# Block products in both MLPs of a two-layer decoder trunk, with the S5 preparation rewritten to run beside them

## The chip, the cores and the metric

One core of one Trainium2 chip runs the whole program. The metric is the device time of one execution in microseconds (us). Median of three runs of the kernel before: 2741.39 us (2741.0 to 2742.24).

## The reference, cut to what matters

Two layers on a sequence of 1024 tokens with 1024 channels. Layer 0 mixes tokens by retention, layer 1 by an S5 state-space layer, and each is followed by an MLP of 2816 inner columns with a causal convolution of width 3 on its gate.

```python
def conv_ffn(h, w_up, conv_w, conv_b, w_down):
    val, gate = jnp.split(h @ w_up, 2, axis=-1)
    gate = lax.conv_general_dilated(gate, conv_w, window_strides=(1,), padding=[(CONV_W - 1, 0)], ...) + conv_b
    return (jax.nn.silu(gate) * val) @ w_down

def reference(x, c, pos, ...):
    ...
        h = rms_norm(x) * (1.0 + sc1) + sh1
        ...                                      # i = 0: retention_mixer, i = 1: s5_mixer
        x = x + g1 * y
        h = rms_norm(x) * (1.0 + sc2) + sh2
        x = x + g2 * conv_ffn(h, ffn_w_up[i], ffn_conv_w[i], ffn_conv_b[i], ffn_w_down[i])
    return rms_norm(x) * final_norm_g
```

The S5 mixer's matrices (powers of complex numbers, cosines and sines of angles) depend on the parameters alone, so they can be prepared while something else runs.

## The kernel before

**Arithmetic.** Every f32 factor is split in a high and a low half, and a product is three TensorE products: high by high, high by low, low by high (`mm3`, L802 to L805). ACT copies the high half of a weight (`whi`), VectorE subtracts it for the low half (`wlo`). A matmul here is a 128x128 block of weights against 512 tokens (128x512).

**Stages in program order.** Retention projection and mixer; MLP 0 from about 917 us; the S5 mixer; MLP 1 from 2025.3 us; final norm. Channels lie on partitions, tokens on the free axis, in two halves of 512.

**MLP 0, plain** (`ffn_plain`, L1629). The 2816 inner columns are 22 pairs of 128 (gate and value). For a pair, gate and value times both token halves are four products of 24 matmuls, 96 in all. `gate_out` copies the gate into the convolution's buffer E, `val_out` does the convolution (L1659 to L1661), silu, product and split (L1668). The down-projection follows in groups of two pairs, nine times, and at last four pairs at once.

**MLP 1, block products** (`ffn`, L1769). The up-projection of a pair is regarded as a 2x2 block product (two halves of the input channels, two halves of the tokens) and done by seven products of 12 matmuls, 84 in all, on sums of blocks: A11, S2, S3, S1, A22, A12, S4 (`Q7`; `pair`, L1821). The activation's sums (`SB.b1`, `SB.t1` and so on) are made once, at normalisation (`steps_s`, L666 to L758, which makes `hs`). After each product `tt` (L1248, VectorE) adds or subtracts its bank: into `u` or `tu`, E, or `t`. The first five pairs (`LEADS`) run while the second token half is still being normalised: two of their seven products were done ahead (`lead`), so five are left. The activations are stored in DRAM (`ff_d`) and loaded again for the down-projection, which goes in six groups (`GROUPS`).

**Weights** come through one queue, class `Stream` (L199). `loads` issues DMAs from SP into raw buffers `wr` (three, plus in MLP 1 one "bonus", `wra`, and one lent, `wrx`, while slots are free). `advance` (L270) makes the block sums: two loads into temporaries (`s1`, `s2`), then four adding DMAs issued by POOL (L284, L285, L287 for two). `split` (L338) makes the halves: ACT copy L368, VectorE subtraction L369 for a block; L354 and L355 for a whole weight of the plain kind. `step`, once per product, moves all of it on:

```python
        def step(self):
            self.now += 1
            self.pump()
            self.pump()
```

**S5 preparation** (`s5_weights`, L1380) is a Python generator in the list `bgq`; every `bg()` issues what stands up to its next `yield`. In MLP 0 it is called in the middle of each product (`mid=bg`) and after it (`tick`). It goes over eight groups in two halves. A half group: two multiplies and an add on POOL (`outer`, the add L128 `ar<-ar`), an angle product and two wraps on POOL (`sev<-sp,cst`, L1424, L1425), four transposes on TensorE (L1429), the angle reduction on VectorE (L1433, L1435, L836, L1437), two sines on ACT, `outer` again, four small products (L1451), and stores. After two halves the block is read back in another order and stored (`t_d`). `p1_d`, `cs_d`, `w1_d`, `t_d` are its outputs, `ar` and `sev` its buffers; `ar` and `aacc` have the same sizes as the temporaries of the block sums.

**Banks.** TensorE writes to eight banks `bk`. `RA` counts them round in MLP 0 and the norms, `ffn` has a counter of its own, `DB`.

## Time and profile before

| | |
|---|---|
| median of three runs | 2741.39 us |
| the profiled execution | 2736.73 us |
| its span, first to last instruction | 2734.6 us |
| TensorE's mean granted clock (1 is full) | 0.992 |
| MLP 0 begins, S5 mixer begins, MLP 1 begins | about 917, 1690, 2025.3 us |
| S5 preparation in MLP 0 | 951 to 1536 us |

The profile names for each engine the time in which it was busy; PE is TensorE, PEld its weight load (which goes on beside the products), DVE VectorE, ACT ScalarE, POOL GpSimd, SP the engine that issues most loads. A row of a view of waits gives the waiting engine and line, what it waited for, the sum, the number of times and the longest. A row of the view of instructions gives line, engine, operation, output and inputs with sizes, the number, and busy time with the mean of one; behind the second bar the idle time before them with who ended it. All rows are from the profiled execution.

### The profile page before, as it was taken

To read this page: it belongs to the slowest core of one execution; us is meant where nothing else is said; L and a number is where in the kernel's file an instruction comes from. 1 tells how busy PE (TensorE), PEld (TensorE's weight loads), DVE (VectorE), ACT (ScalarE), POOL (GpSimd) and SP (SyncE) were. 2 spreads that over 40 slices of the span, in tenths; PEclk is the share of its full clock that TensorE was granted. 3 is DMA by queue.
4 is the path that set the end of the run, shared out by engine and by line. 5 is a ranking of instruction groups with operands and counts; after the bars stand their busy time and mean duration, and the time that the engine had idled before them with its cause. 6 is when DMAs were issued, how large, how long until landed. Compare 5 with 4: busy or idle time off the path is not lost.

```text
span 2734.6 us, 33612 instructions
## 1 busy us (share of the span) xinstructions
PE 2647.9 (97%) x13041; PEld 2224.5 (81%) x13041; DVE 1627.4 (60%) x2254; ACT 856.4 (31%) x1346; POOL 847.3 (31%) x718
## 2 busy tenths in 40 slices
PE   6999999999999999999999999999998999999998
PEld 4798888888888778888888888888876788888887
DVE  8664564755765775666666545664247666666454
ACT  5322131231321343333333223222245434343112
POOL 5445676776100423333333004221122212110004
PEclk8999999999999999999999999999999999999999
DMA  7644335343432132332323213995247866645211
GB/s 246 165 135 143 112 119 165 113 154 116 128 135 77 37 100 82 100 100 92 100 96 100 80 45 123 298 288 168 70 114 167 203 159 165 170 125 207 101 61 62
DMA packets 341819, 357.12 MB, mean 131 GB/s; under 512 B 40444, under 2 KB 279580, under 8 KB 341660
## 3 DMA queue, kind: packets, MB, share of 16 engines
q1 hardware_dynamic: 292028, 269.36, 31.8%
q10 hardware_dynamic: 36960, 62.55, 6.4%
q0 software_dynamic: 12672, 23.07, 4.9%
q8 instruction: 102, 1.67, 0.2%
q14 instruction: 57, 0.47, 0.1%
HBM read 259.82 MB, written 70.42 MB: 121 GB/s over the span
## 4 chain that ended last, share of the span: by engine, by line
PE 74%; DVE 11%; DMA 5%; ACT 4%; issue 2%; POOL 2%; SPq 1%; ACTq 0%; POOLq 0%; DVEq 0%
PE bk L803 23%; PE bk L805 23%; PE bk L804 22%; PE bk L1115 1%; PE bk L1113 1%; PE bk L1114 1%; DVE wlo L355 1%; DMA U<-u_d 1%; POOL ar L128 1%; ACT whi L354 1%; DVE stf L1188 1%; DMA blk<-in_ada_w 1%; PE bk L2181 1%; DVE bacc L497 1%; PE bk L1209 1%
## 5 line engine op out<-in xcount | busy, mean ns | idle before, releaser
L803 PE MATMUL bk<-hh,whi 128*128 128x512 f32 x1344 | 530.5, 395 | 6.7 <-DVE t L1663 2.5
L804 PE MATMUL bk<-hl,whi 128*128 128x512 f32 x1344 | 526.5, 392 | 5.6 <-POOL hl L128 3.1
L805 PE MATMUL bk<-hh,wlo 128*128 128x512 f32 x1344 | 525.5, 391 | 0.3 <-DVE wlo L355 0.3
L355 DVE TENSOR_TENSOR wlo<-wr,whi 128x1024 fp32r<-128x1024 f32 x173 | 243.1, 1407 | 259.8 <-ACT whi L354 259.8
L1507 DVE SCALAR_TENSOR_TENSOR x<-bk,mods,x 128x512 f32<-128x512 f32 x288 | 228.9, 813 | 188.9 <-PE bk L805 188.5
L803 PEld LDWEIGHTS bk<-hh,whi 128*128 128x128 f32 x1344 | 253.8, 189 | 62.2 <-DVE t L1663 2.9
L804 PEld LDWEIGHTS bk<-hl,whi 128*128 128x128 f32 x1344 | 253.8, 189 | 60.4 <-POOL hl L128 5.9
L805 PEld LDWEIGHTS bk<-hh,wlo 128*128 128x128 f32 x1344 | 253.7, 189 | 53.8 <-DVE wlo L355 0.7
L354 ACT ACTIVATE whi<-wr 128x1024 fp32r<-128x1024 f32 x173 | 181.2, 1055 | 273.5 <-PE bk L804 215.7
L803 PE MATMUL bk<-fh,whi 128*128 128x512 f32 (+1 forms) x608 | 232.1, 382 | 0.2 <-DVE t L1663 0.2
L804 PE MATMUL bk<-fl,whi 128*128 128x512 f32 (+1 forms) x608 | 229.8, 378 | 0.0
L805 PE MATMUL bk<-fh,wlo 128*128 128x512 f32 (+1 forms) x608 | 229.8, 378 | 0.0
L128 POOL TENSOR_TENSOR nacc<-nacc,ar 128x512 f32<-128x512 f32 x36 | 46.6, 1295 | 412.1 <-ACT ar L613 411.9
L495 POOL TENSOR_TENSOR aacc<-aacc,ar 128x1024 f32<-128x1024 f32 x70 | 172.4, 2462 | 5.8
L128 POOL TENSOR_TENSOR ar<-sp 128x512 f32<-128x512 f32 (+1 forms) x64 | 80.9, 1279 | 247.7 <-ACT sev L1439 130.6
L1113 PE MATMUL bk<-whi,hh 128*128 128x256 f32 x512 | 147.2, 288 | 0.0
L1115 PE MATMUL bk<-whi,hl 128*128 128x256 f32 x512 | 144.8, 283 | 0.0
L1114 PE MATMUL bk<-wlo,hh 128*128 128x256 f32 x512 | 144.8, 283 | 0.0
L803 PE MATMUL bk<-hs,whi 128*128 128x512 f32 x328 | 129.6, 395 | 8.1 <-DVE E L1248 7.1
L803 PEld LDWEIGHTS bk<-fh,whi 128*128 128x128 f32 x608 | 114.2, 188 | 23.0 <-issue 0.8
L804 PE MATMUL bk<-hs,whi 128*128 128x512 f32 x328 | 129.1, 393 | 3.6 <-DVE hs L695 3.6
L805 PEld LDWEIGHTS bk<-fh,wlo 128*128 128x128 f32 x608 | 114.2, 188 | 21.5
(384 smaller groups left out, 5515.3 us busy)
## 6 DMA issues: line engine op xcount, KB each, us to landing
ar<-in_ada_w SPq DMA_DIRECT2D x80, 512.0 KB, 4.3
wr<-in_ffn_w_up SPq DMA_DIRECT2D x78, 512.0 KB, 3.7
wr<-in_ret_w_in SPq DMA_DIRECT2D x48, 512.0 KB, 4.0
wr<-in_ffn_w_down SPq DMA_DIRECT2D x44, 512.0 KB, 3.4
ff_d<-t ACTq DMA_DIRECT2D x22, 512.0 KB, 4.3
fr<-ff_d SPq DMA_DIRECT2D x22, 512.0 KB, 5.7
blk<-in_ada_w SPq DMA_DIRECT2D x32, 256.0 KB, 6.0
act_d<-sg ACTq DMA_DIRECT2D x16, 512.0 KB, 5.1
```

The source lines that it names most:

```text
L128: GP.tensor_tensor(out=out, in0=in0, in1=in1, op=op)
L354: A.activation(out=hi, in_=r, func=AF.Copy)
L355: low = lambda: V.tensor_tensor(out=lo, in0=r, in1=f(hi), op=ALU.subtract)
L495: eng.tensor_tensor(out=acc, in0=acc, in1=raw, op=ALU.add)
L497: eng.scalar_tensor_tensor(out=acc, in0=raw, scalar=cond[:, kt:kt + 1], in1=acc, op0=ALU.mult, op1=ALU.add)
L803: PE.matmul(bk, lhsT=lh, rhs=rh, start=first, stop=False, skip_group_check=skip)
L804: PE.matmul(bk, lhsT=lh, rhs=rl, start=False, stop=False, skip_group_check=skip)
L805: PE.matmul(bk, lhsT=ll, rhs=rh, start=False, stop=last, skip_group_check=skip)
L1113: PE.matmul(o, lhsT=hh, rhs=wh[:, k % 4, :], start=(k == 0), stop=False)
L1114: PE.matmul(o, lhsT=hh, rhs=wl[:, k % 4, :], start=False, stop=False)
L1115: PE.matmul(o, lhsT=hl, rhs=wh[:, k % 4, :], start=False, stop=(k == 7))
L1507: V.scalar_tensor_tensor(out=dst, in0=bk, scalar=g, in1=src, op0=ALU.mult, op1=ALU.add)
```

## The change

MLP 0 is done by block products too: `ffn(0, finish0, SB, s5_weights())` takes the place of `ffn_plain` (some 135 lines that go away), and the retention projection ends with the same normalisation into blocks as the S5 mixer does (`nrm.start_s`), its new x going to DRAM from ACT's queue.

To run beside that, the S5 preparation is cut anew. The adds of `outer` become adding DMAs issued by POOL; the angle product becomes four ACT copies with a scale; the transposes' result goes through parts of the `ar` buffers; and every `yield` is now one product's step, 26 for a group, where `bg` before was called twice for a product. It is called in `pair` behind the evacuation of the bank, not ahead of it. The preparation starts when MLP 0's normalisation temporaries are free (`begin`, at the fifth pair), and while it runs (`defer`) the low half of a block's weight is issued one product after its high half (`late`). `ff_d` is now one tensor per layer, and RA's counter serves `DB` too.

```diff
@@ weight_list
-        yield from plain_list(0)
+        yield from ffn_list(0)
...
@@ Stream.split, a block's weight
                 A.activation(out=hi, in_=src, func=AF.Copy)
-                V.tensor_tensor(out=lo, in0=src, in1=f(hi), op=ALU.subtract)
...
+                def low():
+                    V.tensor_tensor(out=lo, in0=src, in1=f(hi), op=ALU.subtract)
...
+                    if q in ("A22", "S4"):
+                        self.consume(first + (q == "S4"))
+                        self.loads()
+
+                self.lows.append(low)
+                if not self.defer:
+                    self.late()
+
+        def late(self):
+            if self.lows:
+                while self.lows:
+                    self.lows.pop(0)()
                 self.loads()
                 self.sums(1)
...
         def step(self):
             self.now += 1
-            self.pump()
-            self.pump()
+            self.late()
+            self.try_()
+            self.try_()
...
@@ s5_weights
-        kq = tb[:, HW:T]
+        kq = ev0
...
-                    gp_tt(ta[:, 0:m], ta[:, 0:m], tb[:, 0:m], ALU.add)
-
+                    GP.dma_start(out=ta[:, 0:m], in_=tb[:, 0:m], accum_op=ALU.add)
+
+                for g in range(4):
+                    A.activation(out=ev1[:, g * P:(g + 1) * P], in_=cst[:, C_IDX:C_IDX + P], func=AF.Copy,
+                                 scale=sp[:, O_TH + hf * 4 + g:O_TH + hf * 4 + g + 1])
                 outer(8, O_RR, O_RI, O_Y1, O_Y2, True)
...
-                gp_tt(ev1.rearrange("p (g c) -> p g c", g=4), thv, cv, ALU.mult)
...
@@ the retention projection's last block
-            hT = []
+            SB = Blocks()
...
+                    if hf:
+                        A.dma_start(out=x_d[m], in_=xs[m])
...
-                nrm.start(hf, xs, 0, 3, hT, 6, 7)
+                nrm.start_s(hf, xs, 0, 3, SB, 6, 7)
...
@@ pair
             def next_(i):
                 W.step()
+
+            def behind_(i):
+                after(i)
                 bg(steps * (2 if i == 6 else 1))
...
             tt(u, u, b2, ALU.add)
             free_bank(b2)
-            after(1)
+            behind_(1)
...
@@ begin
-                if ff > 1 and not W.busy(stmp) and not W.bonus_busy:
+                if ff and not W.busy(stmp) and not W.bonus_busy:
                     W.retired = None
                     bgq.append(behind)
                     behind = None
+                    W.defer = True
...
@@ the end of ffn's up-projection
+        W.defer = False
         xs[:] = xin
-        DB = Rot(list(pb))
+        DB = RA
+        RA.ids, RA.i = list(pb), 0
...
-    bgq.append(s5_weights())
-    ffn_plain(0, finish0)
+    ffn(0, finish0, SB, s5_weights())
```

What each engine is given, in order, in MLP 0 (names without their buffer numbers; `t_7740` and `t_7741` are the convolution's result and its silu, line numbers of the change are its own).

VectorE, before, from one value product to the next: convolution, product, split, then one whole weight's low half.

```order
L1659 TENSOR_SCALAR t_7740<-E,prm 128x512
L1660 SCALAR_TENSOR_TENSOR t_7740<-E,prm,t_7740 128x512
L1661 SCALAR_TENSOR_TENSOR t_7740<-E,prm,t_7740 128x512
L1663 TENSOR_TENSOR t_7741<-t_7741,bk 128x512
L1668 TENSOR_TENSOR fl<-t_7741,fh 128x512
L355 TENSOR_TENSOR wlo<-wr,whi 128x1024
```

VectorE, now, in a pair of the middle of MLP 0, from the first sum of the pair's banks to the first step of its convolution; L358 is the low half of a block's weight, L839 and L1433 are S5's.

```order
L839 TENSOR_SCALAR sev<-sev 128x512
L1433 SCALAR_TENSOR_TENSOR sev<-sev 128x512
L358 TENSOR_TENSOR whi<-sq,whi 128x512
L358 TENSOR_TENSOR wlo<-wr,wlo 128x512
L1251 TENSOR_TENSOR tu<-tu,bk 128x512
L358 TENSOR_TENSOR whi<-sq,whi 128x512
L1251 TENSOR_TENSOR E<-tu,bk 128x8x64
L358 TENSOR_TENSOR wlo<-wr,wlo 128x512
L1251 TENSOR_TENSOR E<-E,bk 128x8x64
L358 TENSOR_TENSOR whi<-wr,whi 128x512
L1251 TENSOR_TENSOR E<-tu,bk 128x8x64
L1673 SCALAR_TENSOR_TENSOR t_7741<-E,prm,t_7741 128x512
```

A low half now stands ahead of nearly every evacuation of a bank; before, one of twice the size stood behind each two.

POOL, before, the S5 preparation alone: one half group from its first `outer` to the end of its second.

```order
L128 TENSOR_TENSOR db<-db,cst 16x128
L128 TENSOR_TENSOR ar<-sp 128x4x8x16 x2
L128 TENSOR_TENSOR ar<-ar 128x512
L128 TENSOR_TENSOR sev<-sp,cst 128x512
L1424 TENSOR_SCALAR ar<-sev 128x512
L1425 TENSOR_SCALAR ar<-ar 128x512
L128 TENSOR_TENSOR ar<-sp 128x576 x2
L128 TENSOR_TENSOR ar<-ar 128x576
L128 TENSOR_TENSOR ar<-ar,db 16x2x16 x2
```

POOL, now, the same half group; L268, L269 and L271 are the adding DMAs of the block sums, L1420 those of `outer`.

```order
L128 TENSOR_TENSOR db<-db,cst 16x128
L128 TENSOR_TENSOR ar<-sp 128x4x8x16 x2
L1420 DMA ar<-ar 128x512
L1426 TENSOR_SCALAR sev<-sev 128x512
L1427 TENSOR_SCALAR sev<-sev 128x512
L271 DMA sq<-wr 128x512
L268 DMA sq<-wr 128x512
L269 DMA wr<-wr 128x512
L128 TENSOR_TENSOR ar<-sp 128x576 x2
L1420 DMA ar<-ar 128x576
L271 DMA sq<-sq 128x512
```

The two adds and the angle product have left POOL's order, and the issues of six adding DMAs stand in the same stretch.

SP, in MLP 1, before (the change leaves this order as it is): two pairs' loads.

```order
L243 DMA wr<-in_ffn_w_up 128x8x128
L243 DMA wra<-in_ffn_w_up 128x8x128
L276 DMA sq<-in_ffn_w_up 128x4x128 x2
L243 DMA wrx<-in_ffn_w_up 128x8x128
L243 DMA wr<-in_ffn_w_up 128x8x128
L276 DMA aacc<-in_ffn_w_up 128x4x128 x2
```

SP, now, in MLP 0: two pairs' loads with the S5 preparation's between them.

```order
L227 DMA wr<-in_ffn_w_up 128x8x128 x2
L260 DMA sq<-in_ffn_w_up 128x4x128 x2
L1392 DMA sp<-s5p_d 128x808
L1394 DMA db<-in_s_d 16x128
L1471 DMA ar<-ks_d 16x8x128 x8
L227 DMA wr<-in_ffn_w_up 128x8x128 x2
L260 DMA sq<-in_ffn_w_up 128x4x128 x2
```

MLP 0's raw weights go through the three `wr` buffers alone and its sums through one pair of temporaries (`sq`), where MLP 1 goes round five buffers and two pairs (`sq`, `aacc`).

## Rows read from the trace of the kernel before

**Rows 1.** Busy time of each engine, share of the span, number of instructions

```profile
PE 2647.9 (97%) x13041; PEld 2224.5 (81%) x13041; DVE 1627.4 (60%) x2254; ACT 856.4 (31%) x1346; POOL 847.3 (31%) x718
```

**Rows 2.** Stretches: length, PE, PEld, DVE, ACT, POOL busy, PEclk, DMA share, GB/s

```profile
917.30:960.00 42.70, 37.78 (x171) 30.67 (x172) 32.92 (x39) 15.69 (x24) 20.08 (x19) 1.00 0.12 35
960.00:1530.00 570.00, 567.43 (x2573) 462.37 (x2572) 352.16 (x435) 196.45 (x294) 183.10 (x177) 1.00 0.30 96
...
2025.30:2160.00 134.70, 116.18 (x483) 91.40 (x482) 97.50 (x149) 68.44 (x120) 38.72 (x41) 0.96 0.74 173
2160.00:2440.00 280.00, 280.00 (x1237) 231.86 (x1236) 178.84 (x267) 115.23 (x208) 50.00 (x57) 1.00 0.66 161
...
2080.00:2160.00 80.00, 70.72 (x297) 56.54 (x298) 56.99 (x88) 34.11 (x62) 17.61 (x20) 0.98 0.87 204
```

**Rows 3.** Waits of PE, 2025.3 to 2160 us; then 917.3 to 1540 us

```profile
PE bk L803 <- DVE E L1248: 10.7, 6, 2.4
...
PE bk L1429 <- POOL ar L128: 1.4, 2, 1.0
...
PE bk L1451 <- POOL ar L128: 0.7, 1, 0.7
```

**Rows 4.** Timeline from 2090.5 us: start, duration, engine, line, [idle before, releaser]

```profile
2090.80 0.86 POOL L287 DMA_DIRECT2D aacc<-wr  x1 [0.69 <-DVE whi L369]
...
2096.05 0.63 ACT L368 ACTIVATE whi<-aacc 128x512 fp32r<-128x512 f32 x1 [4.89 <-DMA aacc<-wr]
2096.71 0.69 DVE L369 TENSOR_TENSOR whi<-aacc,whi 128x512 fp32r<-128x512 f32 x1 [1.80 <-ACT whi L368]
...
2098.91 0.69 DVE L369 TENSOR_TENSOR wlo<-sq,wlo 128x512 fp32r<-128x512 f32 x1 [1.50 <-ACT wlo L368]
...
2100.34 0.47 PE L803 MATMUL bk<-hs,wlo 128*128 128x512 f32 x1 [2.36 <-DVE E L1248]
```

**Rows 5.** DMA: a queue's share; issues, KB, median us to landing; 2160 to 2440, last row 2080 to 2160

```profile
q0 software_dynamic: 8154, 14.84, 30.8%
...
wr<-in_ffn_w_up SPq DMA_DIRECT2D x16, 512.0 KB, 3.7
...
sq<-sq POOLq DMA_DIRECT2D x7, 256.0 KB, 3.3
...
wr<-wr POOLq DMA_DIRECT2D x6, 256.0 KB, 5.7
...
wr<-in_ffn_w_up SPq DMA_DIRECT2D x8, 512.0 KB, 5.7
```

**Rows 6.** Instructions of DVE, 960 to 1530 us (busy us, mean ns | idle before)

```profile
L1660 DVE SCALAR_TENSOR_TENSOR t<-E,prm,t 128x512 f32<-128x512 f32 x35 | 33.2, 949 | 1.3
...
L1668 DVE TENSOR_TENSOR fl<-t,fh 128x512 fp32r<-128x512 f32 x36 | 29.6, 822 | 25.1 <-ACT fh L1667 25.1
L1433 DVE SCALAR_TENSOR_TENSOR sev<-ar,sev 128x512 f32<-128x512 f32 x32 | 27.2, 850 | 11.3 <-POOL ar L1425 10.8
...
L836 DVE TENSOR_SCALAR sev<-sev 128x512 f32<-128x512 f32 x16 | 6.8, 426 | 0.6
```

**Rows 7.** Instructions of DVE, 2160 to 2440 us

```profile
L1809 DVE SCALAR_TENSOR_TENSOR t<-E,prm,t 128x512 f32<-128x512 f32 x30 | 22.6, 752 | 1.1
...
L369 DVE TENSOR_TENSOR whi<-sq,whi 128x512 fp32r<-128x512 f32 x16 | 11.0, 688 | 0.0
```

**Rows 8.** Instructions of POOL, 960 to 1530 us

```profile
L128 POOL TENSOR_TENSOR ar<-sp 128x576 f32<-128x576 f32 (+1 forms) x62 | 78.7, 1283 | 247.7 <-ACT sev L1439 130.6 <-ACT ar L1474 74.2 <-PE bk L1429 26.5
L128 POOL TENSOR_TENSOR ar<-ar 128x576 f32<-128x576 f32 (+1 forms) x31 | 47.7, 1538 | 2.4
L128 POOL TENSOR_TENSOR sev<-sp,cst 128x512 f32<-128x512 f32 x15 | 20.1, 1342 | 0.0
```

**Rows 9.** Instructions of POOL, 2160 to 2440 us

```profile
L287 POOL DMA_DIRECT2D sq<-sq x7 | 6.1, 871 | 22.8 <-DVE t L1248 8.5 <-DVE tu L1248 4.9 <-DMA sq<-wr 4.9
```

## What I expect of the change

> **What bounds the kernel now.** I read the busy shares first: TensorE is busy for 97% of the span, VectorE for 60%, the others for a third [rows 1]. So time goes away only where TensorE gets less work or waits less. Next, the table of stages [rows 2]. It gives the price of a matmul and two kinds of stage. In MLP 1 from 2160 to 2440 us, block products with weights prepared far ahead, TensorE never stops: 1237 matmuls in 280.00 us, 0.2264 us each. In MLP 0, 960 to 1530 us, the plain products beside the S5 preparation leave it 2.6 us idle in 570. The poor stage is the first 135 us of MLP 1 (2025.3 to 2160): 483 matmuls at 0.2264 are 109.4 us, so 25.3 us are lost there. The plain MLP 0 begins far cheaper: 42.7 us for 171 matmuls (38.7 us), 4.0 us lost [rows 2].
>
> The waits say what is lost at MLP 1's beginning: 10.7 of the 25.3 us are "PE waits for DVE E", six times, 2.4 us at most [rows 3]. The timeline shows where one comes from [rows 4]. An adding DMA on POOL's queue is issued at 2090.80; the ACT copy of its sum (the high half) begins at 2096.05, after 4.89 us idle; VectorE's low half waits for that copy, then for the next one; behind the two stands the block difference E, and TensorE goes on at 2100.34, 2.36 us late. So the reader should keep one chain in mind: load, adding DMA, ACT copy, VectorE low half, E, TensorE. VectorE takes its instructions in order, so a late sum delays an E that has nothing to do with it.
>
> **The change part by part.**
>
> *Matmuls.* Each of MLP 0's 22 column pairs now takes 84 matmuls of 128x512 instead of 96; down-projection and the S5 preparation keep theirs. 22 x 12 = 264, and the order's PE rows fall from 12041 to 11777, which is 264. At 0.2264 us [rows 2]: **-59.8 us**. They stood on a path with hardly any idle time, so all of it counts.
>
> *MLP 0's beginning.* It becomes the code that MLP 1 has now: same groups, same normalisation into blocks, same five pairs of five products. The retention projection ahead of it gives VectorE less to do than MLP 1's predecessor, but its last half is as long, so I take MLP 1's loss for the plain one's: 25.3 - 4.0 = **+21.3 us** [rows 2]. Bounds: +8 (only the 12.8 us of the five pairs, below, with the entry as cheap as the plain one) and +30.
>
> *The other 17 pairs.* Two things differ from MLP 1's good stretch. First, depth. MLP 0 has three raw weight buffers, since the S5 preparation needs the slots and the "ar" buffers; MLP 1 borrows two more (wra, wrx in the order's SP rows). By the Stream's rules the second load of a pair is then issued four products before the ACT copy of its first sum, in MLP 1's good stretch ten. Second, company. The adds and loads take 0.66 of the DMA engines in MLP 1; the old MLP 0 took 0.30 [rows 2], about half of it S5's; 32 more adding DMAs (8.7 MB, at 0.308 of 280 us for 14.84 MB [rows 5] some 50 us of a 566 us stretch) bring the sum to about 0.66 + 0.15 + 0.09 = 0.90, an estimate. The nearest row is MLP 1's beginning, 2080 to 2160: 0.87 [rows 2]. VectorE goes from 0.64 (178.84 of 280 us) by about 0.10 for S5's rows (four lines, the first 27.2 and the last 6.8 us, 56.1 together over 16 half groups, nine of them now in some 323 us) and about 0.09 because its SBUF operations beside a computing POOL take 949 and 822 ns instead of some 750 and 690 [rows 6, 7], to about 0.83: not the bound.
>
> The chain in MLP 0: load 3.7 to 5.7 us, add 5.7, copy 0.62, low half 0.69, in sum 10.7 to 12.7 us [rows 4, 5]. One product is 12 x 0.2264 = 2.72 us. The copy stands four products (10.9 us) behind the load, the low half five, because it is now issued one product later (13.6 us), and the E behind it is not waited for before about two products more. So the usual chain is covered, and what TensorE loses is the tail: pairs where a POOL burst of the preparation or a long landing adds over 5 us. Bounds for a pair: 0, as in MLP 1's good stretch, and 2.6 us, as in the five lead pairs (80 us for 297 matmuls, 67.2 us, 12.8 lost, 297/60 pairs) [rows 2]. The kernel is nearer to the first, since the deferred low half alone gives back 2.72 us, more than the longest wait of E there (2.4 [rows 3]). I take 0.4 us a pair: **+7 us** (0 to +44).
>
> *S5 preparation.* Per half group POOL loses two adds (1.54 us each) and the angle product (1.34), in sum 4.4, and gets two DMA issues (0.87 each) [rows 8, 9]; ACT gets four 128x128 copies in place of the angle product. All beside other work: POOL is idle two thirds of the old stretch. What matters is when TensorE needs the sum: its transposes and small products stand in its own queue. The first sum has four products (10.9 us) for two multiplies (2.6), an issue (0.9) and a landing of 3.3 to 5.7: covered. The second multiplies wait for the transposes that read the same buffer, and have about three products (8.2 us) for 6.8 to 9.2: up to 1 us late, nine times under the up-projection. Now these waits are 2.1 us in all [rows 3]. I take **+2 us** (-2 to +13). If the load v or an add falls behind one of these POOL bursts the pair pays, which is in the term above.
>
> *Rest.* The activations go through DRAM as in MLP 1 (22 stores and loads), and VectorE has 5 x 16 accumulations in the middle instead of 9 x 16: off the path, as MLP 1's down-projection has no listed wait of this kind. The x stores stand on ACT's queue in the last half of the retention projection, as they do before MLP 1. The preparation, spread over products, runs to the end of the fifth down group; its tail is then drained at once, but S5 starts some 60 us later. The one bank counter changes bank numbers, not order. In MLP 1 the order of VectorE is unchanged, and low halves are not deferred there. Together 0 (-1 to +2).
>
> Sum: -59.8 + 21.3 + 7 + 2 = -29.5 us. The profiled execution took 2736.73 us, so 2707; the median of the runs shown is 2741.39, 4.7 us more, and I carry the difference over: **2712 us**.
>
> **The rivals.**
>
> *The short lead decides (slower).* Every one of the 17 pairs loses what MLP 1's lead pairs lose, 2.6 us, and the second sums are 8 us late in all: -59.8 + 21.3 + 44 + 8 = +13.5, **2755 us**. For it: the same lead of four products, and a DMA share of 0.87 there [rows 2]. Against it: no pair there had deferred low halves, and they had five products to hide in, not seven. It decides from (59.8 - 21.3 - 2)/17 = 2.1 us a pair. The Trainium skill (SBUF — State Buffer, "SBUF: two separate sides") speaks for it: a DMA issued by GpSimd has its descriptors written through a port that VectorE can hold, and the page has one at 3.1 instead of 0.62 us beside a VectorE copy. With two such adds in a row a chain would be some 5 us longer by that, an estimate from the page, about as much as the cover. The rows here bear it out only in part: issues of 0.87 us [rows 9] and medians of 3.3 and 5.7 to landing beside a VectorE that was busy for 64% [rows 2, 5].
>
> *Half of it.* 1.3 us a pair and 5 us for the sums: -11.5, **2730 us**. For it: the DMA share of 0.90 is an average, and both bursts are periodic, 7 products against 26, so every phase comes up.
>
> *Full cover.* No pair waits and the preparation's waits go: -59.8 + 21.3 - 2 = -40.5, **2701 us**. For it: 0 idle in 280 us of MLP 1 [rows 2]. Against: that is with ten products of lead.
>
> *That nothing is saved* is excluded: the 264 matmuls are gone from the order.
>
> **How the numbers follow.** Chances: forecast 0.45, full cover 0.28, half 0.15, short lead 0.12. With the entry at its bounds (-13, +9) the forecast and full cover span 2688 to 2721; half and its neighbours reach 2742. The range 2688 to 2742 leaves out most of the short lead's chance and a little below. 0.2% is 5.5 us, about what a measurement here can tell from no change. Faster: 0.45 + 0.28 + half of the rest that stays below 2736, in sum 0.82; slower: the short lead, 0.12; between them 0.06.
>
> **What the profile after would show.** PE MATMUL 264 fewer; MLP 0 some 30 us shorter. About 25 us lost in its first 135 us, with "PE waits for DVE E" and ACT waiting for sums. In the pairs after the fifth few waits, under 1 us a pair; a DMA share near 0.9; VectorE near 0.83. Small waits of the transposes and of the small products for the adding DMA instead of POOL. MLP 1 and S5 as before. I am wrong if E is waited for in most late pairs (short lead), if the beginning loses much less than 25 us, or if time appears outside MLP 0.

## The result: slower by 0.6%, and the profile after

The changed kernel took 2759.7 us (median of four runs, 2754.42 to 2762.41) against 2741.72 us of the kernel before: a ratio of 1.0059 with a 95% interval of 1.0047 to 1.0071. I had forecast 2712, range 2688 to 2742. The profiled execution took 2754.42 us, 17.7 more than that of before.

The 264 matmuls did go: the page's row of busy times, beside [rows 1], has 12777 matmuls instead of 13041 and 32 us less of TensorE.

```profile
PE 2615.8 (95%) x12777; PEld 2188.5 (80%) x12777; DVE 1673.6 (61%) x2359; ACT 949.3 (34%) x1562; POOL 878.1 (32%) x789
```

The table of stages for TensorE alone (length, busy us and matmuls, granted clock, DMA share, GB/s), which answers to [rows 2]; first the kernel before, over the stretches in which the two can be laid beside each other:

```profile
917.30:960.00 42.70, 37.78 (x171) 1.00 0.12 35
960.00:1060.00 100.00, 99.30 (x450) 1.00 0.30 97
1060.00:1380.00 320.00, 319.18 (x1449) 1.00 0.30 97
1380.00:1700.00 320.00, 318.68 (x1439) 1.00 0.28 90
```

and the changed kernel:

```profile
917.30:960.00 42.70, 35.53 (x149) 0.92 0.55 138
960.00:1060.00 100.00, 90.15 (x381) 0.98 0.79 184
1060.00:1380.00 320.00, 292.67 (x1277) 0.96 0.81 199
1380.00:1700.00 320.00, 301.15 (x1336) 0.97 0.52 165
```

What a stretch loses is its length less busy time times granted clock. Before, that is 5.6 us up to 1060, 0.8 up to 1380 and 1.3 up to 1700. After, it is 21.7 (the five lead pairs), 39.0 (some 15 of the 17 other pairs, 2.6 us each) and 27.9 (the last pairs and the down-projection with the rest of the S5 preparation). Of the 39.0 us, 27.3 are idle time and the rest is the lower clock. The difference is 81 us; less the 59.8 of the missing matmuls 21, against 17.7 measured (the clock column has two digits, worth 3 us here). MLP 1 is as it was: its good stretch, 2178 to 2458 us now, has 1237 matmuls in 280.00 us again. The whole loss lies in MLP 0.

The waits of TensorE there (waiting line, what for: us, times, longest), 1060 to 1380 us and then 1380 to 1700, where [rows 3] had 2.1 us for the preparation; L1251 is VectorE's evacuation of a bank, L1436 the preparation's transposes, and "issue" means that the profile shows nothing that the engine waited for:

```profile
PE bk L806 <- DVE E L1251: 19.4, 6, 6.7
PE bk L806 <- ACT whi L353: 5.2, 1, 5.2
PE bk L1436 <- DMA ar<-ar: 1.7, 1, 1.7
PE bk L1436 <- issue: 1.0, 1, 1.0
...
PE bk L1436 <- issue: 13.1, 3, 8.2
PE bk L806 <- DVE E L1251: 4.4, 3, 3.2
```

Who waits ahead of that stands in the view of all engines' waits, 1060 to 1380 us:

```profile
POOL wr L269 <- DMA wr<-in_ffn_w_up: 65.8, 11, 11.3
...
ACT whi L353 <- DMA sq<-sq: 21.7, 6, 6.0
DVE wlo L358 <- ACT wlo L353: 21.2, 11, 4.8
...
DVE sev L1430 <- POOL sev L1427: 17.9, 6, 5.5
```

VectorE stands 17.9 us before the preparation's angle, which POOL has not wrapped yet. What leads to TensorE's longest wait, in the timeline (start, duration, engine):

```profile
1243.41 3.64 DVE L1673 SCALAR_TENSOR_TENSOR t<-E,prm,t 128x512 f32<-128x512 f32 x1 [2.84 <-ACT E L1663]
1243.67 2.87 POOL L128 TENSOR_TENSOR ar<-sp 128x512 f32<-128x512 f32 x2
...
1247.87 0.73 ACT L1677 ACTIVATE t<-t,prm 128x512 f32<-128x512 f32 x1 [3.88 <-DVE t L1674]
...
1249.95 1.27 ACT L1423 ACTIVATE sev<-cst,sp 128x128 f32<-128x128 f32 x4
...
1251.31 0.61 POOL L1426 TENSOR_SCALAR sev<-sev 128x512 f32<-128x512 f32 x1 [3.48 <-ACT sev L1423]
...
1252.66 0.69 DVE L1430 SCALAR_TENSOR_TENSOR sev<-sev 128x512 f32<-128x512 f32 x1 [1.89 <-POOL sev L1427]
1253.19 2.72 POOL L128 TENSOR_TENSOR ar<-sp 128x576 f32<-128x576 f32 x2
1253.27 3.21 DVE L358 TENSOR_TENSOR wlo<-wr,wlo 128x512 fp32r<-128x512 f32 x1
...
1262.51 0.68 DVE L1251 TENSOR_TENSOR E<-tu,bk 128x512 f32<-128x512 f32 x1
...
1263.34 0.77 PE L806 MATMUL bk<-hs,whi 128*128 128x512 f32 x1 [6.70 <-DVE E L1251]
```

A convolution step of VectorE lasts 3.64 us beside the preparation's multiplies, and ACT's silu waits 3.88 us for the step behind it; behind the silu stand the four copies of the angle (L1423). POOL waits 3.48 us for these copies, VectorE 1.89 for POOL, then a low half lasts 3.21 us beside POOL's next multiplies, and every E behind them is late. Only this low half belongs to the reader's chain from load to TensorE, and it is held up neither by a load nor by a sum.

Such a stop costs twice. TensorE stood for 6.70 us up to 1263.34, and in the ten us from 1260 the granted clock was 0.54, near the lower of its two levels (1.2 of 2.4 GHz):

```profile
1250.00:1260.00 10.00, 6.64 (x32) 0.95 0.47 102
1260.00:1270.00 10.00, 6.66 (x17) 0.54 1.01 252
1270.00:1280.00 10.00, 10.00 (x49) 1.00 0.85 220
```

### The profile page after: what moved, and what is told of

The parts are those of the page before. It is cut to its first block, busy times and chain, and to the rows that moved or that the text cites. A ratio compares the mean times of both kernels' runs of the same rounds, so it can differ in the third digit from the quotient of the medians.

```text
span 2752.6 us, 34099 instructions
## 1 busy us (share of the span) xinstructions
PE 2615.8 (95%) x12777; PEld 2188.5 (80%) x12777; DVE 1673.6 (61%) x2359; ACT 949.3 (34%) x1562; POOL 878.1 (32%) x789
## 4 chain that ended last, share of the span: by engine, by line
PE 38%; DMA 5%; DVE 4%; issue 4%; ACT 2%; POOL 2%; SPq 0%; ACTq 0%; POOLq 0%; DVEq 0%
PE bk L806 12%; PE bk L808 12%; PE bk L807 12%; POOL ar L128 1%; DMA sq<-sq 1%; DVE t L1251 1%; DMA t_d<-ar 1%; DMA sq<-in_ffn_w_up 1%; PE bk L2054 0%; DVE z L2062 0%; DMA fr<-ff_d 0%; DMA W<-w_d 0%; ACT ar L1475 0%; DVE wlo L358 0%; DMA wr<-in_ffn_w_up 0%
## 5 line engine op out<-in xcount | busy, mean ns | idle before, releaser
L806 PE MATMUL bk<-hs,whi 128*128 128x512 f32 x656 | 264.0, 402 | 31.3 <-DVE E L1251 21.3
L807 PE MATMUL bk<-hs,whi 128*128 128x512 f32 x656 | 262.0, 399 | 6.3 <-DVE hs L698 4.7
L808 PE MATMUL bk<-hs,wlo 128*128 128x512 f32 x656 | 259.8, 396 | 0.0
L806 PE MATMUL bk<-hh,whi 128*128 128x512 f32 x640 | 254.2, 397 | 4.4 <-ACT hh L971 1.7
L339 DVE TENSOR_TENSOR wlo<-wr,whi 128x1024 fp32r<-128x1024 f32 x126 | 173.1, 1378 | 137.0 <-ACT whi L338 136.0
L807 PE MATMUL bk<-hl,whi 128*128 128x512 f32 x640 | 252.3, 394 | 3.1 <-POOL hl L128 1.8
L808 PE MATMUL bk<-hh,wlo 128*128 128x512 f32 x640 | 252.0, 394 | 0.2 <-DVE wlo L339 0.2
L806 PE MATMUL bk<-hs,wlo 128*128 128x512 f32 x576 | 229.1, 398 | 22.9 <-DVE E L1251 22.9
L808 PE MATMUL bk<-hs,whi 128*128 128x512 f32 x576 | 228.0, 396 | 0.0
L807 PE MATMUL bk<-hs,wlo 128*128 128x512 f32 x576 | 227.3, 395 | 0.5 <-DVE hs L698 0.5
L338 ACT ACTIVATE whi<-wr 128x1024 fp32r<-128x1024 f32 x126 | 131.4, 1056 | 276.3 <-PE bk L807 217.7
L807 PE MATMUL bk<-fl,whi 128*128 128x512 f32 (+1 forms) x480 | 180.6, 376 | 0.0
L806 PEld LDWEIGHTS bk<-hs,whi 128*128 128x128 f32 x656 | 126.9, 193 | 64.3 <-issue 11.3
L807 PEld LDWEIGHTS bk<-hs,whi 128*128 128x128 f32 x656 | 126.8, 193 | 34.2 <-DVE hs L698 6.1
L806 PEld LDWEIGHTS bk<-hs,wlo 128*128 128x128 f32 x576 | 109.5, 190 | 51.4 <-ACT wlo L353 13.0
L808 PEld LDWEIGHTS bk<-hs,wlo 128*128 128x128 f32 x656 | 126.1, 192 | 26.7
```

Of the source, the lines that this page charges most:

```text
L338: A.activation(out=hi, in_=r, func=AF.Copy)
L339: low = lambda: V.tensor_tensor(out=lo, in0=r, in1=f(hi), op=ALU.subtract)
L806: PE.matmul(bk, lhsT=lh, rhs=rh, start=first, stop=False, skip_group_check=skip)
L807: PE.matmul(bk, lhsT=lh, rhs=rl, start=False, stop=False, skip_group_check=skip)
L808: PE.matmul(bk, lhsT=ll, rhs=rh, start=False, stop=last, skip_group_check=skip)
```

## The experiments

Theory A, formed on this profile: crossed queues. The preparation's waits stand in the orders of VectorE, ACT and POOL between the MLP's instructions, and its links have one product (2.7 us) each. Theory B is the rival of the prediction: the weights' lead of four products is too short. Theory C: too many transfers.

A ratio behind a time is against the kernel before in the same runs, with its 95% interval. The expectations speak of the stretch from 1100 to 1500 us. The rows shown here end at 1380 us, which leaves out the end of the up-projection and the beginning of the down-projection; where the two stretches tell different things, both are given. The change itself was not run again beside these kernels, so a difference from it is one between two ratios, each with its interval; for y1, y2, x7 and w1 the intervals overlap.

### Without the preparation, and four single edits

**x1_held.** `begin` keeps the generator, and the down-projection starts it:

```diff
+        held_back = []
...
-                    bgq.append(behind)
+                    held_back.append(behind)
...
         W.defer = False
+        bgq.extend(held_back)
```

> The S5 preparation is held back and begins only with the down-projection of MLP 0; buffers, raw weight slots and the deferred low halves stay as in the change. Look at the stretch 1100 to 1500 us, where the change leaves TensorE idle for 37 us of 400. Theory A (crossed queues: the preparation's waits stand in the orders of VectorE, ACT and POOL between the MLP's own instructions): with the preparation gone from there the idle time falls under 5 us and the granted clock back to 1.00. Theory B (short lead: load, add, copy and low half do not fit in four products): it stays at 30 us or more. The whole time says nothing of either: what is left of the preparation is run at the end of the down-projection and costs, by the 26 steps of a group, some hundreds of us.

The one execution took 2930.18 us, as most of the preparation now runs with nothing beside it. In the stretch in question (length, TensorE busy, clock, DMA share, GB/s):

```profile
1060.00:1380.00 320.00, 320.00 (x1414) 1.00 0.67 170
```

No idle time at all, as theory A said. (Up to 1500 us it is 5.6, 3.5 of them a wait of the first transposes and 2.0 one for the down-projection's weights.) But one thing was not kept as the expectation has it: the slot that the generator's buffer takes in the change stayed free here, and the weight queue borrowed it as a fourth raw buffer (six loads of `wrx` from 1060 to 1380 us). So this run alone doesn't decide against theory B; z2_slow, below, has the change's three.

**x2_wraps.** The two wraps ahead of the outer product on POOL:

```diff
-                outer(8, O_RR, O_RI, O_Y1, O_Y2, True)
                 GP.tensor_scalar(out=kq, in0=ev1, scalar1=INV_2PI, scalar2=MAGIC, op0=ALU.mult, op1=ALU.add)
                 GP.tensor_scalar(out=kq, in0=kq, scalar1=-MAGIC, scalar2=1.0, op0=ALU.add, op1=ALU.mult)
+                outer(8, O_RR, O_RI, O_Y1, O_Y2, True)
```

> One exchange on POOL: the two wraps of the angle (0.6 us each) are issued ahead of the outer product (two multiplies and an adding DMA, some 3.8 us) instead of behind it, so VectorE's first angle step no longer waits for the outer product. Same instructions. Theory A: VectorE's wait for the second wrap (30.2 us over 11 times between 1000 and 1510 us) falls under 10 us, and of the time some 10 to 25 us go: 2735 to 2750. Theory B: nothing changes for the weights: 2755 to 2764.

2792.83 us, ratio 1.0195 (1.0167 to 1.0223): worse by 33 us, and neither theory expected that. TensorE's waits, 1060 to 1380 and 1380 to 1700 us:

```profile
PE bk L1436 <- DMA ar<-ar: 15.5, 4, 7.1
PE bk L806 <- DVE E L1251: 12.4, 4, 5.1
PE bk L1436 <- issue: 8.9, 2, 4.4
...
PE bk L1436 <- issue: 17.4, 3, 7.4
PE bk L1436 <- DMA ar<-ar: 11.0, 4, 3.6
```

VectorE's wait for POOL fell from 30.2 to 12.8 us (1000 to 1510 us; under 10 expected) and the waits for E with it, 19.4 to 12.4; the transposes, whose sum now starts later on POOL, went from 16.2 to 52.8 over the two stretches. At this place the preparation has no slack: what VectorE no longer waits for, the transposes do.

**x6_nodefer.**

```diff
-                    W.defer = True
```

> Low halves are issued right behind their high half, as in MLP 1 (no deferral). Theory A: deferral is beside the point or helps a little where ACT is held up; 2755 to 2775. Theory B: the chain loses one product of cover, 2.7 us, in each of 17 pairs where it was already too short; 2775 to 2800. If deferral itself were the fault (a low half that stands ahead of an evacuation), it would be faster: 2735 to 2750.

2766.31 us, 1.0087 (1.0072 to 1.0102): some 7 us slower than the change. Deferral helps by a little, not by one product in each pair.

**x7_pooladd.**

```diff
-                    GP.dma_start(out=ta[:, 0:m], in_=tb[:, 0:m], accum_op=ALU.add)
+                    gp_tt(ta[:, 0:m], ta[:, 0:m], tb[:, 0:m], ALU.add)
```

> The 32 adding DMAs of the outer products are POOL adds again (1.54 us each), all else as in the change. Theory C (too many transfers: the DMA engines, 0.8 busy, make all sums late): faster by over 10 us, under 2750. Theory A: POOL's run of work ahead of the wraps grows by some 0.7 us and its queue holds the block sums longer, but the transposes no longer wait for a landing: 2755 to 2770. Theory B: 2755 to 2764.

2763.14 us, 1.0076 (1.0061 to 1.0091), 3 us from the change, with a DMA share of 0.74 instead of 0.81 from 1060 to 1380 us: 32 transfers less gave nothing. Theory C falls for these transfers.

### The waits one at a time

**y1_angle.**

```diff
                 yield True
+                yield True
                 for c_ in (TWO_PI_1, TWO_PI_2, TWO_PI_3):
                     V.scalar_tensor_tensor(out=ev1, in0=kq, scalar=-c_, in1=ev1, op0=ALU.mult, op1=ALU.add)
-                    yield True
+                    if c_ != TWO_PI_2:
+                        yield True
```

> VectorE's first angle step is issued two products behind POOL's wraps instead of one, and the second and third share a step, so that a half group keeps its length; POOL's order and the transposes stay as in the change. Theory A, part 1 (VectorE stands in its order before wraps that POOL has not made yet, and E behind it is late): VectorE's wait for POOL in 1000 to 1510 us falls from 30 to under 12 us, TensorE's wait for E from 26 to under 16, and the time by 8 to 20 us, to 2740 to 2752. If VectorE's wait was beside the point: 2757 to 2763.

2753.33 us, 1.0052 (1.0034 to 1.0071). From 1000 to 1510 us VectorE's wait fell from 30.2 to 10.2 us as expected, TensorE's for E only from 26.3 to 22.0, and the transposes' rose from 12.6 to 16.1.

**y2_stores.** The two `A.dma_start(out=ks_d...)` stand behind the half group's last `yield` instead of ahead of it.

> The two small stores of a half group (ks_d, issued by ACT behind a POOL add that waits for ACT's own copy) are issued one product later, so ACT's queue no longer stands before POOL's add; no step more. Theory A, part 2 (ACT's high halves wait behind these stores: the waits of 5.2 us at 1077 and 5.4 us at 1191): these two kinds go, and 5 to 15 us of the time: 2745 to 2755. If they only swap places with another wait: 2757 to 2763.

2754.36 us, 1.0055 (1.0036 to 1.0074). The waits of 5.2 and 5.4 us became 4.4 and 3.7; other ones grew, and 30.3 us of waits for E stood where 26.3 had. With the change at 1.0059, y1 and y2 alone are within its interval.

**y3_td.**

```diff
-            for _ in range(6):
+            for _ in range(4):
                 yield True
...
             A.dma_start(out=t_d[j], in_=tb)
-            yield True
+            for _ in range(3):
+                yield True
```

> At the end of a group the copy and store of t_d are issued two products earlier and the next group begins two products after them instead of at once: the same 26 steps. Theory A, part 3 (POOL's first multiplies of a group stand before the store of t_d, 13 us in five groups, and wraps, VectorE and transposes behind them): transposes wait under 5 us instead of 12.6 and the time falls by 5 to 12 us, 2748 to 2755. Against it: the copy now waits on ACT for the eight loads, and holds high halves back: 2757 to 2770.

2745.37 us, 1.0019 (1.0005 to 1.0033): 14 us back, the best of the three, though the transposes still waited 10.7 us, not under 5. In the trace the gain lies from 1380 to 1700 us (TensorE busy for 305.49 instead of 301.15 us); beside the block products up to 1380 it is idle for 26.4 us where the change has 27.3.

**y4_all.** The three together.

> The three edits together (with the read-back of ks_d one product later, since its stores are). Theory A: the parts add up, TensorE's idle time in 1100 to 1500 us falls from 37 to under 15 us, and the time to 2715 to 2740. If TensorE only waits for the next link of the preparation each time: 2745 to 2765.

2739.04 us, 0.9996 (0.9984 to 1.0007): the loss against the kernel before is gone, 20 us in all, so the parts add up roughly, and the time is at the slow end of what theory A gave. The idle time is not: 24.9 us from 1100 to 1500 us, where under 15 were expected. From 1060 to 1380 us TensorE is still idle for 20 us:

```profile
PE bk L806 <- DVE E L1251: 11.8, 5, 5.1
PE bk L806 <- ACT sev L1445: 5.0, 2, 2.8
PE bk L1455 <- DMA ar<-ar: 2.3, 1, 2.3
```

### The pace

**z2_slow.** Steps behind four of seven products, two a bank in the down-projection:

```diff
-                bg(steps * (2 if i == 6 else 1))
+                if i in (1, 3, 5, 6):
+                    bg(steps * (2 if i == 6 else 1))
...
                     tick(2)
+                    if True:
+                        bg(1)
```

> Order inside the preparation as in the change, but slower beside the block products: its steps go on behind four of a pair's seven products (the 2nd, 4th, 6th and 7th) instead of all, and in the down-projection, where no block sums are made, two steps a bank instead of one. Theory A (its links stand in the other queues because each has only 2.7 us): in 1100 to 1500 us the idle time falls from 37 to under 15 us; some of it comes back as waits of the transposes in the down-projection (1500 to 1700 us, 4 us now, up to 25); time 2725 to 2745. If it is the amount of company and not its pace (port, DMA engines), idle per group stays at some 8 us and the time falls only by the share moved: 2740 to 2755.

2802.26 us, 1.0229 (1.0212 to 1.0246). The time is 60 us worse than the kernel before and no theory had it; in the expectation's stretch, 1100 to 1500 us, TensorE is idle for 38.7 us, as the faster steps of the down-projection begin in it. But beside the block products the loss is gone, as theory A said. TensorE's row 1060 to 1380 us, and its waits from 1380 to 1700:

```profile
1060.00:1380.00 320.00, 318.03 (x1428) 260.02 (x1427) 223.10 (x317) 156.62 (x284) 98.88 (x113) 1.00 0.79 197
...
PE bk L1436 <- DMA ar<-ar: 45.2, 7, 21.1
PE bk L1436 <- issue: 22.9, 3, 15.2
```

(columns as in [rows 2]). Idle 2.0 us where the change has 27.3, with the DMA share at 0.79 where the change has 0.81, VectorE busy for 223 us where the change has 211, and POOL for 99 of 110 us. It has the change's three raw buffers and its four products of lead (no load of `wrx` or `wra` beside the preparation), so theory B falls here. Neither the lead nor the DMA engines' load nor VectorE's stopped TensorE by itself. The company is not halved either: POOL does 22 multiplies of outer products in this stretch where the change has 28, a fifth less, for a loss that all but goes. What z2_slow changes is how soon each link of the preparation is asked for, and also behind which products (none behind A11, S3 and A22); these two aren't separated. What I mis-sized is the other end: two steps a bank is more than the chain can do.

**z3_slow_all.** The same pace in y4_all.

> The slower pace of the run above together with the three edits of y4_all. Theory A: both remedies act on the same waits, so they don't add up in full: idle under 8 us in 1100 to 1500 us, time 2710 to 2735. If what is left in y4_all (28 us of idle in that stretch) is the port or the DMA engines: idle some 14 us, half the density, 2725 to 2740.

2789.01 us, 1.0181 (1.0165 to 1.0197); idle 2.4 us up to 1380, the loss in the down-projection again. Neither the 2710 to 2735 us nor the idle time expected from 1100 to 1500 us (36.9 us for under 8) came.

**z4_down.** y4_all with `if hf: bg(1)` behind the down-projection's `tick(2)`.

> y4_all with three steps for two banks in the down-projection instead of two: tells what the faster pace there costs or gives by itself. 2733 to 2745; if the drain at the end of the middle groups still cost something in y4_all, 3 to 6 us less than y4_all in the same runs.

2768.64 us, 1.0099 (1.0081 to 1.0117): 30 us slower than y4_all, with 280.95 us busy from 1380 to 1700 instead of 307.22. The expected 2733 to 2745 is missed: one and a half steps a bank is already more than the chain takes, even without block sums beside it.

**z1_split.** z4_down with a step between the two multiplies of an outer product, one more ahead of the transposes, the sines ahead of the second outer product, 30 steps a group (the first of these edits shown):

```diff
                     gp_tt(ta[:, 0:m].rearrange(pat, g=4, k=n), av, yv, ALU.mult)
+                    yield True
                     gp_tt(tb[:, 0:m].rearrange(pat, g=4, k=n), bv, zv, ALU.mult)
```

> As z4_down, and POOL's bursts are cut: the two multiplies of an outer product are issued one product apart, the transposes one product later, the sines beside the transposes; 30 steps a group instead of 26. VectorE's instructions that stretch to over 3 us beside two multiplies in a row are then shorter, and adding DMAs of the block sums come in between. If the bursts on POOL hold what y4_all still loses: idle in 1100 to 1500 us from 25 to under 14 us and 2715 to 2735; if not, 2735 to 2750.

2750.83 us, 1.0037 (1.0025 to 1.0049), at the far end of the range for the case that the bursts do not hold it; the idle time from 1100 to 1500 us is 33.5 us, where under 14 was expected if they do. Idle from 1060 to 1380 us 10.2 instead of y4_all's 20.4, but 27.3 us of waits of the transposes afterwards, where z4_down has 33.9. Cut bursts and slower pace came together here, so which of them gave the 10 us isn't separated.

### The bank

All six waits for E from 1060 to 1380 us in the changed kernel stand at the same place: each ends with the first E of a pair (in the timeline the one behind `tu`'s second sum), and product A22 goes on accumulating in the bank that this E reads, S3's, with only one product, S1, between.

**w1_fresh.**

```diff
-            tt(g1, as_sel(u, chalf), as_sel(b4, chalf), ALU.subtract)
+            g0 = E[:, 2:10, 0:64]
+            tt(g0, as_sel(u, chalf), as_sel(b4, chalf), ALU.subtract)
+            free_bank(b4)
...
-            tt(g1, g1, as_sel(b3, chalf), ALU.subtract)
+            tt(g1, g0, as_sel(b3, chalf), ALU.subtract)
...
-            product(b4, q("A22"), SB.t4, False)
+            b5 = new_bank()
+            product(b5, q("A22"), SB.t4, True)
             next_(4)
-            tt(E[:, 2:10, 0:64], as_sel(u, chalf), as_sel(b4, chalf), ALU.subtract)
-            free_bank(b4)
+            tt(g0, g0, as_sel(b5, chalf), ALU.subtract)
+            free_bank(b5)
```

> One bank's dependence is taken away, in both MLPs: in the change the product A22 goes on accumulating in the bank of S3 and so may not begin before VectorE has read that bank (E), one product after S3; here A22 gets a bank of its own, E's lower half takes u less S3 first and A22 after it. Same number of matmuls and VectorE operations; the preparation's order and pace as in the change. If the exposure is that bank (theory A in its final form: lateness of up to 2.7 us is harmless everywhere but there): TensorE's wait for E falls from 19 to under 6 us in 1060 to 1380 us, MLP 1's first 130 us lose 10 us less too, and the time falls by 25 to 45 us, to 2715 to 2735. If lateness is larger than any bank can hide: waits move on to the weights (TensorE waits for copies or low halves) and the time stays within 8 us, 2751 to 2762.

2749.41 us, 1.0035 (1.0023 to 1.0048): 10 us less than the change, where 25 to 45 were expected. The two profiled executions (2755.68 and 2754.42 us) lie closer together, so the traces show where the waits went and not the 10 us. TensorE's waits, 1060 to 1380 us:

```profile
PE bk L1436 <- DMA ar<-ar: 9.4, 4, 3.6
PE bk L806 <- DVE E L1251: 5.3, 4, 2.6
PE bk L1436 <- issue: 4.1, 3, 1.9
PE bk L1453 <- DMA ar<-ar: 1.5, 2, 0.8
```

E fell to 5.3 as said, so the bank was where lateness came through. But the transposes now wait 13.5 us instead of 2.7; that a TensorE which no longer stops at the bank reaches them earlier fits, and isn't shown. The waits for E that are left, four here, all end with the second E of a pair. It reads the bank of S1, in which product S4 goes on accumulating: the next place of the same kind. In MLP 1's first 135 us nothing was gained where 10 us were expected: TensorE waits 10.8 us for E, four times, instead of 11.0, seven times.

**w2_fresh_all** (with the edits of y4_all):

> The bank of its own together with the three edits of y4_all. Theory A: what is left are the transposes at group changes: 2700 to 2722. If not: 2730 to 2742, as y4_all.

2740.63 us, 1.0003 (0.9993 to 1.0013): no better than y4_all.

**w3_fresh_all_nodefer** (and without `W.defer = True`):

> As w2_fresh_all with low halves right behind their high halves: in the change deferral gave some 7 us (x6_nodefer). If it gave them by sparing E, it gives nothing now: within 4 us of w2_fresh_all. If by the weights' chain: 5 to 10 us slower than it.

2751.02 us, 1.0034 (1.0020 to 1.0048): 10 us slower. Deferral is worth about the same whether or not A22 has a bank to itself, so it doesn't work by sparing that one bank alone. Without deferral TensorE's waits for E did grow, from 19.4 to 27.7 us in x6_nodefer and from 2.7 to 5.4 here (1060 to 1380 us); what else it gives time to, the weights' chain perhaps, isn't shown.

**w4_before_fresh** (the same edit in the kernel before):

> The kernel before with the same edit (its MLP 1 alone does block products): what the bank is worth without the preparation beside it. MLP 1's first 135 us lose 25 us, 10.7 of them as waits for E: 2728 to 2736. If the lead pairs only wait for the next thing: 2738 to 2742.

2741.52 us, 1.0006 (0.9996 to 1.0015): nothing. In MLP 1's first 135 us TensorE still waits for E (before: 10.7 us, six times, three of them at S3's bank):

```profile
PE bk L803 <- DVE E L1248: 11.8, 4, 5.8
```

All four now end with the second E, S1's bank. In a lead pair only product A22 stands between S1 and S4, so this bank has as little cover as the first.

### Two versions with all of it

**v1_wraps_pooladd** is w1_fresh with the edits of x2 and x7, and of y2 and y3 as in y4_all; **v2_angle_pooladd** has y1 in place of x2.

> All that the runs point to, at full pace: A22's own bank, the two stores and t_d moved as in y4_all, the wraps ahead of the outer product, and POOL adds in place of the adding DMAs of the outer products (so that the transposes wait 1.54 us for a sum and not 3.3 to 6 us for a landing). If what is left at full pace is the length of the preparation's own chain (waits of the transposes for the adding DMA: 14 us in w1_fresh, 20 in w2_fresh_all between 1060 and 1720 us): these fall under 8 us and the time to 2715 to 2733, faster than both kernels. If VectorE, held by 1.5 us more of POOL work per outer product, takes its place: 2738 to 2755.

> The same with the late angle step of y1_angle in place of the exchanged wraps, so the outer product keeps its place at the head of POOL's work. If the start of the outer product decides for the transposes: 4 to 10 us faster than v1; if the adding DMA's landing was all: within 4 us of it. 2710 to 2733; 2738 to 2755 if POOL's adds hold VectorE too long.

v1 took 2751.5 us, 1.0036 (1.0024 to 1.0048), v2 2740.27 us, 0.9992 (0.9983 to 1.0002). Between the two the order of POOL's work decides, by 11 us, as v2's expectation had it. The 2710 to 2733 us hoped for did not come; both lie in the range given for POOL's adds holding VectorE, and VectorE is busy for 229 and 245 us from 1060 to 1380 where w2_fresh_all has 223. In v1 TensorE waits at the transposes, now for POOL's add; in v2 for E, all three times the second E of a pair (TensorE's waits, 1060 to 1380 us, of v1 and then of v2):

```profile
PE bk L1436 <- POOL ar L128: 19.0, 7, 4.7
PE bk L806 <- DVE E L1251: 1.7, 2, 1.2
```

```profile
PE bk L806 <- DVE E L1251: 11.4, 3, 4.3
PE bk L1438 <- POOL ar L128: 0.5, 1, 0.5
```

None of the eighteen kernels is faster than the kernel before beyond its interval.

## Why the prediction was wrong

**Right.** The matmuls (-59.8 us: 264 gone, 13041 to 12777 in the traces). The beginning: 21.7 - 5.6 = 16 us for the 21.3 forecast, 9.4 of it waits for E, as in MLP 1. MLP 1 and the S5 mixer unchanged. The DMA share came out at 0.81 (0.90 forecast). VectorE's share did not: 0.66 (211 of 320 us) where 0.83 was forecast, so the loss is not one of VectorE's load.

**The step that failed: "The other 17 pairs", +7 us.** They lost 2.6 us each, 39 us up to 1380 alone. Two sentences of that step carried the error.

- "The E behind it is not waited for before about two products more." It is waited for after one: A22 accumulates in S3's bank. w1_fresh took 14 of 19 us of these waits away, though only part of the time. I had worked out the cover of a weight's copy and low half, and took the cover of E from the same count instead of following the bank.
- "What TensorE loses is the tail: pairs where a POOL burst of the preparation or a long landing adds over 5 us." I treated the two chains as independent and each as covered by itself. Each of the three engines takes its instructions in order, and both chains pass through all of them; in the timeline above, multiplies of the preparation hold a convolution step, this the silu, the silu the angle's copies, these POOL and POOL VectorE, until TensorE stands for 6.70 us. With the preparation away (x1_held) TensorE is idle for 0 us of 320, with it asked for less often (z2_slow) for 2.0, in the change for 27.3. In MLP 1's good stretch [rows 2], from which I took the lower bound, there is no second chain.

**The second step: "S5 preparation", +2 us, "All beside other work".** With the old, plain products that was so at a higher pace: 2.6 us idle in 570 [rows 2], with 36 multiplies of outer products from 1060 to 1380 us where the change has 28. In the change the transposes alone waited 16 us, for 14 of which the profile names no releaser, and the stretch with the down-projection lost 27.9. I priced instructions that left POOL (4.4 us a half group) and not what the new steps leave each link to be ready in, one product.

**The rival that had the time had the wrong cause.** The short lead gave 2755 us from 2.6 us a pair, and 2.6 is what was measured; z2_slow shows that the lead alone costs nothing (2.0 us idle in 320), and x1_held, with a buffer more, the same without any company. What it needed was the company, which in my rivals stood only as bursts of "half of it". Its number came from MLP 1's lead pairs, where E is waited for at the same kind of place, three times at S3's bank and three at S1's. That the sizes agree proves nothing about the mechanism.

**What stays open.** At four steps a pair the company is all but free beside the block products, at seven it is not, and waits removed there came back in part as others. y4_all, w2_fresh_all and v2_angle_pooladd all end at 2739 to 2741 us, some 28 us above the forecast's sum. What sets that level is not separated: the preparation's own chain against MLP 0's length, VectorE's long instructions beside POOL's multiplies, the second bank (S1's), or several of these. A preparation with less work or an earlier start was not tried, nor the slower steps beside the block products with the old pace in the down-projection.

## What to carry to other kernels

When background work is laid beside a dense stage, ask of each link how late it may come, and follow it through each engine's order and to the bank or buffer that TensorE needs next; busy shares of 0.6 to 0.8 say nothing about that. Measure the stage once without the background and once with it at a slower pace: these two runs told more here than the edits of its order. And when a stage is shortened, look at what was hidden under the time that goes: removing a wait only helps if the next link of the hidden chain is ready by then.

## What the runs showed of the hardware

VectorE's instructions with two inputs in SBUF stretch beside POOL's multiplies: the low half above took 3.21 us beside two multiplies of 2.72 together, against 0.68 alone, and ended 0.57 us behind them; the convolution step of 3.64 us ended 0.51 behind its two. E, which reads one input from a bank, kept its 0.68 at 1050.97 us, inside two multiplies that lasted from 1050.41 to 1053.77. The Trainium skill (SBUF — State Buffer, "SBUF: two separate sides") says that VectorE and GpSimd (POOL) share a pair of ports which goes to one of them for a whole instruction, and that agrees. In the prediction I had entered it as an average (949 and 822 ns for some 750 and 690 [rows 6, 7]); it is a few instructions of three microseconds, which is what a queue behind them feels.

The Trainium skill's warning in the same section, on DMAs issued by GpSimd beside a VectorE copy (3.1 us for 0.62), is not what the change's trace shows from 1060 to 1380 us: POOL's issues of adding DMAs took 0.85 to 1.2 us, and in z2_slow TensorE was idle for 2.0 us with as many of them for the block sums (58 in both). No run here took VectorE's share in a single landing apart.
